# A hybrid encoder layer: input products of un-normalised h, the norm's factor applied after PSUM

## The chip, the cores and the metric

The kernel runs on one core of a Trainium2 chip. A core has five engines with queues of their own: TensorE (PE: matrix products and transposes, into PSUM), VectorE (DVE), ScalarE (ACT), GpSimd (POOL), and SyncE (SP), which here issues all DMAs. SBUF is the on-chip memory; PSUM holds the results of products in banks. The metric is device microseconds (us) of one execution; lower is better.

## The reference

One layer on h, 16 meta tokens and 512 tokens of 1024 channels, all float32:

```python
u = rmsnorm(h, norm_mix)                      # h * rsqrt(mean(h*h) + eps) * gain
proj = u @ w_in
gates = sigmoid(proj[..., C_RW + C_FX:] + b_gate)
y_rw = rwkv7_branch(proj[..., :C_RW], ...)    # f + mu * (token_shift(f) - f), then a recurrence over tokens
y_fx = fox_branch(proj[..., C_RW:C_RW + C_FX], ...)   # q, k normed per head; softmax attention with forgetting
merged = gates[..., :1024] * (y_rw @ w_out_rw) + gates[..., 1024:] * (y_fx @ w_out_fx)
h = h + merged @ w_o
h = h + square(relu(rmsnorm(h, norm_mlp) @ w_up)) @ w_down
```

The factor of rmsnorm is one number for each token, and a product is linear in u; so it can be applied to h before the product, or to each column of the product after it.

## The kernel before

Channels lie on partitions, tokens along the free dimension (528 columns, two halves of 264). A product in float32 accuracy is made of three passes: every operand is split into a high part and a remainder (`uhi`/`ulo` for u, `whi`/`wlo` for a weight block of 128 outputs), and hi·hi, hi·lo and lo·hi add up in one PSUM bank. A block of the input projection is thus 8 x 3 products for each half of the tokens.

**Front.** x arrives in two halves of tokens. It is scaled by the norm's gain and split; with this un-normalised split the eight forget logits (`pf`) and two blocks, the inputs of the low-rank decay (`B_LORA`) and of the output gate (`B_GD`), are multiplied (`proj`), and `rs`, the norm's factor, is made from the squares (`pss`). Then h is multiplied by `rs` and split a second time, into the same `uhi`, `ulo` (lines 369 to 376). All later blocks use this one. The two first blocks become `lhi`/`llo` after tanh; the first recurrent product, `pup` (line 682), reads them.

**Middle.** 24 blocks for four pairs of heads (FoX q, k, v and recurrent k, r, v for each) and 16 gate blocks, taken by `projections` from a list in order of rank (recurrent 1, FoX 2, gates 9). A FoX or recurrent block has two parts of 264 columns, a q or gate block one of 512. Each part goes to one of two PSUM banks named pj; a function `evac` takes it out. For a recurrent block `evac` is the token shift (`tshift`, lines 300 and 301): ACT writes the product times mu, shifted by one token, and DVE adds the product times 1-mu; both read PSUM. A gate is written to DRAM and read back at the output projection.

For each of two groups of two pairs the recurrence goes: decay (`pup`), norm of the keys (`pkk`), scores of chunks of 64 tokens (`psr`, into `Bm` and `L`), keys turned (`pbt`), the inverse of a triangular matrix for each chunk (`inverse`: 15 substitution steps on DVE for blocks of 16, then products `pw`, `pw2`), then `chain`, nine steps that depend on each other (`pch`, `pyy`), and group norm (`pyt`, `pg`). FoX attention of one pair goes over four blocks of 128 queries: scores (`psc`), softmax on DVE and ACT, transposes (`ppt`, `ppm`), and the mix (`py`).

**What sets the order.** PE's order in the middle is written out when the program is built: `Turns` picks, by rank, the stream whose next products are ready by the estimates of `Clock`, and otherwise goes on with a product of the projection. `Clock` estimates each instruction by engine, fixed cost and size. The other engines' orders come from the framework's scheduler, with `high_priority` for ranks 0 and 1. Engines run in order; waits are semaphores.

**Output projection and the rest.** For each of eight blocks m of 128 channels, two gates are loaded (`gl`, two buffers for each branch), go through tanh, and multiply the products `po` (DVE, line 1036); POOL adds the two branches (line 1038), and ACT and DVE split the sum (lines 1039, 1040). Then come `w_o`, the second norm and the MLP, in which PE's order is that of the code.

## Time and profile before

| | us |
|---|---|
| median of 3 runs (lowest to highest) | 927.95 (926.56 to 931.89) |
| the profiled execution | 923.5 |
| its span | 921.7 |
| busy PE / weight loads / DVE / ACT / POOL | 872.5 / 709.4 / 523.7 / 424.9 / 159.9 |
| front: to the first recurrent product | 41.3 |
| middle: to the first product of the output projection | 475.3 |
| output projection, w_o, MLP | the rest, 446.4 |

The profile names an instruction by line, engine and `output<-inputs`, with a count (x4). PE is busy nearly all the time by the page, but a product's end is modelled, and small products and half a clock count as busy too; so the table of stretches is read together with the waits. "PEclk" is the share of full clock that PE was granted. In a list of waits stand the waiting engine, tile and line, the releaser after the arrow, total us, number and longest.

### The profile page before, as it was taken

The page shows a single profiled execution, that of the slowest core. Times are in us where ns is not written, and L with a number is a line of the kernel's source. Part 1 is how long each engine was busy: PE and PEld are TensorE (multiplying, and loading weights), DVE is VectorE, ACT ScalarE, POOL GpSimd, SP SyncE. Part 2 cuts the span into 40 slices and gives each one's busy share as a digit, 9 for nine tenths or more (in the row PEclk, how much of TensorE's full clock was granted, in tenths as well). Part 3 has the DMA queues.
Part 4 walks back from the last instruction along what each step waited for, and adds up shares of the span by engine and source line. Part 5 has one row for each costly group of instructions (what it writes and reads, how often), then busy time and mean ns, then how long its engine had stood idle before and what let it go on. Part 6 is the DMA issues. An engine that isn't in the chain of part 4 may idle for free.

```text
span 921.7 us, 15446 instructions
## 1 busy us (share of the span) xinstructions
PE 872.5 (95%) x5964; PEld 709.4 (77%) x5964; DVE 523.7 (57%) x1052; ACT 424.9 (46%) x887; POOL 159.9 (17%) x145
## 2 busy tenths in 40 slices
PE   6589898999998999999989999999999999999998
PEld 4587785768896777676768878988888888888886
DVE  7966885465887893565387664454423245452322
ACT  7755352686465533674465553344322234442221
POOL 4253433123343352112102100000000000000000
PEclk9889998999999999999989999999999999999999
DMA  6121204022111142211266540132323232322331
GB/s 207 46 71 47 69 27 132 25 71 70 50 46 59 47 133 70 69 60 47 69 229 205 183 160 1 58 103 92 101 94 101 94 102 93 100 95 94 123 116 57
DMA packets 45449, 83.30 MB, mean 90 GB/s; under 512 B 5048, under 2 KB 6200, under 8 KB 45376
## 3 DMA queue, kind: packets, MB, share of 16 engines
q1 hardware_dynamic: 45376, 82.32, 26.8%
q8 instruction: 47, 0.77, 0.3%
q14 instruction: 26, 0.21, 0.1%
HBM read 75.99 MB, written 6.31 MB: 89 GB/s over the span
## 4 chain that ended last, share of the span: by engine, by line
PE 76%; DVE 15%; DMA 3%; ACT 3%; issue 2%; POOLq 0%; POOL 0%; SPq 0%; DVEq 0%; ACTq 0%
PE po L1117 19%; PE pd L1150 19%; PE pj L472 18%; PE po L1083 2%; PE po L1034 2%; PE pw L824 2%; PE psc L576 1%; PE py L621 1%; DVE tmp L806 1%; DMA wraw<-in_wup 1%; DVE AX L818 1%; DVE xt L373 1%; PE pbt L772 1%; DVE AX L807 1%; DMA wraw<-in_win 1%
## 5 line engine op out<-in xcount | busy, mean ns | idle before, releaser
L233 DVE TENSOR_TENSOR wlo<-wraw,whi 128x512 fp32r<-128x512 f32 x148 | 107.0, 724 | 171.6 <-ACT whi L232 170.1
L232 ACT CAST whi<-wraw 128x512 fp32r<-128x512 f32 x152 | 93.8, 620 | 190.4 <-PE pd L1150 109.6
L472 PE MATMUL pj<-uhi,whi 128*128 128x264 f32 (+1 forms) x480 | 168.5, 351 | 9.5 <-DVE orr L301 4.7
L472 PE MATMUL pj<-uhi,wlo 128*128 128x264 f32 (+1 forms) x480 | 156.3, 326 | 0.0
L472 PE MATMUL pj<-ulo,whi 128*128 128x264 f32 (+1 forms) x480 | 156.3, 326 | 0.0
L444 POOL TENSOR_TENSOR wlo<-wraw,whi 128x512 fp32r<-128x512 f32 x80 | 109.1, 1367 | 216.8 <-ACT whi L443 201.4
L472 PEld LDWEIGHTS pj<-uhi,whi 128*128 128x128 f32 x480 | 92.4, 192 | 30.6 <-issue 10.9
L1150 PE MATMUL pd<-whi,fhi 128*128 128x512 f32 x256 | 99.6, 389 | 0.0
L1150 PE MATMUL pd<-wlo,fhi 128*128 128x512 f32 x256 | 99.6, 389 | 0.0
L1150 PE MATMUL pd<-whi,flo 128*128 128x512 f32 x256 | 99.6, 389 | 0.0
L472 PEld LDWEIGHTS pj<-uhi,wlo 128*128 128x128 f32 x480 | 92.6, 193 | 7.2
L472 PEld LDWEIGHTS pj<-ulo,whi 128*128 128x128 f32 x480 | 92.7, 193 | 4.3
L1117 PE MATMUL po<-zhi,whi 128*128 128x512 f32 (+1 forms) x248 | 94.8, 382 | 0.0
L1117 PE MATMUL po<-zlo,whi 128*128 128x512 f32 (+1 forms) x248 | 94.8, 382 | 0.0
L1117 PE MATMUL po<-zhi,wlo 128*128 128x512 f32 (+1 forms) x248 | 94.8, 382 | 0.0
L443 ACT CAST whi<-wraw 128x512 fp32r<-128x512 f32 x80 | 49.4, 618 | 51.9 <-PE pj L472 27.5
L1150 PEld LDWEIGHTS pd<-whi,fhi 128*128 128x128 f32 x256 | 48.0, 188 | 10.1
L1150 PEld LDWEIGHTS pd<-wlo,fhi 128*128 128x128 f32 x256 | 48.0, 188 | 10.0
L1150 PEld LDWEIGHTS pd<-whi,flo 128*128 128x128 f32 x256 | 48.0, 188 | 9.9
L1117 PEld LDWEIGHTS po<-zlo,whi 128*128 128x128 f32 x248 | 46.6, 188 | 9.1
L1117 PEld LDWEIGHTS po<-zhi,whi 128*128 128x128 f32 x248 | 46.6, 188 | 9.0
L1117 PEld LDWEIGHTS po<-zhi,wlo 128*128 128x128 f32 x248 | 46.6, 188 | 9.0
(279 smaller groups left out, 1455.6 us busy)
## 6 DMA issues: line engine op xcount, KB each, us to landing
wraw<-in_win SPq DMA_DIRECT2D x84, 256.0 KB, 2.6
wraw<-in_wup SPq DMA_DIRECT2D x64, 256.0 KB, 2.6
wraw<-in_wdn SPq DMA_DIRECT2D x64, 256.0 KB, 2.6
gd<-gt SPq DMA_DIRECT2D x16, 256.0 KB, 2.1
wraw<-in_wout SPq DMA_DIRECT2D x16, 256.0 KB, 3.3
gl<-gd SPq DMA_DIRECT2D x16, 256.0 KB, 3.1
wraw<-in_wo SPq DMA_DIRECT2D x16, 256.0 KB, 3.2
xt<-in_ht SPq DMA_DIRECT2D x8, 264.0 KB, 4.7
```

The lines of the kernel that those rows point to most:

```text
L232: A.copy(hi, raw)
L233: low.tensor_tensor(lo, raw, hi.bitcast(F32), ALU.subtract)
L373: V.scalar_tensor_tensor(xt[t][:, k, :], xt[t][:, k, :], pr[:, C_GN + k:C_GN + k + 1], rss[t], ALU.mult, ALU.mult)
L443: A.copy(hi, raw)
L444: G.tensor_tensor(lo, raw, hi.bitcast(F32), ALU.subtract)
L472: mm(po, a, b[:, k, a0:a1], start=n == 0, stop=n == 23)
L576: mm(sc, q[hs, 128 * i:128 * i + 128], k[hs, a:b], start=True, stop=True)
L824: mm(ps_[hs, n - b0, :], lhs(n)[hs], rhs(n)[hs], start=True, stop=True)
L1034: mm(po, a, b[:, k, :], start=n == 0, stop=n == 11)
L1083: mm(po, a[:, k, 128 * i:128 * i + 128], b[:, k, :], start=n == 0, stop=n == 23)
L1117: mm(po[:, t0:t1], a, b[:, k, t0:t1], start=n == 0, stop=n == 23)
L1150: mm(pd[i], a[:, b_, 128 * i:128 * i + 128], b, start=b_ == 0 and n == 0, stop=b_ == 15 and n == 2)
```

## The change

h times gain is split once and used un-normalised by all input products; the second pass over h and its split are gone. The factor `rs` stays in SBUF for all 528 tokens and is applied after PSUM: in the token shift (DVE, then ACT and DVE over 528 columns), on FoX q, k and v (POOL), and on the gates when they are read back (POOL, before tanh). Every part leaves PSUM by one ACT copy. In the front the two first blocks and the forget logits are multiplied together, channel block by channel block, with the weights loaded between the pieces of x; the four weight differences there go from POOL to DVE. `manual_schedule`, which keeps PE's order as written, now spans the front too.

In the planner, a DVE operation in SBUF alone costs 0.2 more and a transpose half as much. In the inverse, four of the eight final copies go from DVE to ACT, the products wait for the pieces that they read instead of for the whole tile, and other streams get turns between the substitution steps. The tile `dg` shares a buffer with `lc`, and the keys are turned before the next pair's decay.

```diff
-                    cost = n / 600 if big else n / 1200
+                    cost = n / 600 if big and not x.is_transpose else n / 1200
...
+                    if eng == "DVE" and not any(a.tensor.space == PSUM for a in ins + outs):
+                        fixed += 0.2
...
-        def tshift(blk, dst):
-
-            tm = rp.tile([128, 1 + T], F32, name="tm")
-            V.memset(tm[:, 0:1], 0.0)
+        def tshift(blk, dst, **kw):
+
+            raw = rp.tile([128, 1 + T], F32, **(kw or dict(name="tm")))
+            V.memset(raw[:, 0:1], 0.0)
+
+            def finish():
+                f = raw[:, 1:]
+                V.tensor_tensor(f, f, rs, ALU.mult)
+                act(dst, f, AF.Copy, scale=pr1[:, blk:blk + 1])
+                V.scalar_tensor_tensor(dst, raw[:, :T], pr[:, C_MU + blk:C_MU + blk + 1], dst, ALU.mult, ALU.add)
 
             def evac(po, sl):
-                act(tm[:, sl.start + 1:sl.stop + 1], po, AF.Copy, scale=pr[:, C_MU + blk:C_MU + blk + 1])
-                V.scalar_tensor_tensor(dst[:, sl], po, pr1[:, blk:blk + 1], tm[:, sl], ALU.mult, ALU.add)
+                A.copy(raw[:, 1 + sl.start:1 + sl.stop], po)
+                return finish if sl.stop == T else None
             return evac
+
+        manual = st.enter_context(ExitStack())
+        manual.enter_context(tc.manual_schedule(engines={mybir.EngineType.PE}))
...
+            def load_x(t, c):
+                nc.sync.dma_start(xt[t][:, 2 * c:2 * c + 2, :].rearrange("p a b -> p (a b)"), ht[t, c])
+            load_x(0, 0)
+            w2 = [[], []]
+            for j in range(2):
+                for i, blk in enumerate((B_LORA, B_GD)):
+                    w2[i].append(load_h(win[blk][:, 512 * j:512 * j + 512], V, "w", (4, 4, 4)))
+                load_x(0, 1 + j)
+            load_x(0, 3)
             for c in range(4):
-                nc.sync.dma_start(xt[0][:, 2 * c:2 * c + 2, :].rearrange("p a b -> p (a b)"), ht[0, c])
-            w_lora = load_w(win[B_LORA], (G, G))
-            for c in range(4):
-                nc.sync.dma_start(xt[1][:, 2 * c:2 * c + 2, :].rearrange("p a b -> p (a b)"), ht[1, c])
-            w_gd = load_w(win[B_GD], (G, G))
+                load_x(1, c)
...
-            rss = []
+            V.tensor_scalar(pr1, pr[:, C_MU:C_MU + 14], -1.0, 1.0, ALU.mult, ALU.add)
+            shifts = [tshift(12 + blk, lfs[i], name="tl", tag="ov", bufs=2) for i, blk in enumerate((B_LORA, B_GD))]
             for t in range(2):
                 tk = slice(HT * t, HT * t + HT)
-                for c in range(4):
-                    sq = xp.tile([128, 2, HT], F32, name="sq", bufs=3)
-                    act(sq, xt[t][:, 2 * c:2 * c + 2, :], AF.Square)
-                    for k in range(2 * c, 2 * c + 2):
-                        gn = pr[:, C_GN + k:C_GN + k + 1]
-                        act(uhi[:, k, tk], xt[t][:, k, :], AF.Copy, scale=gn)
-                        V.scalar_tensor_tensor(ulo[:, k, tk], xt[t][:, k, :], gn, uhi[:, k, tk].bitcast(F32), ALU.mult, ALU.subtract)
-                    if c == 0:
-                        acc = xp.tile([128, HT], F32, name="acc")
-                        V.tensor_tensor(acc, sq[:, 0, :], sq[:, 1, :], ALU.add)
-                    else:
-                        for k in range(2):
-                            V.tensor_tensor(acc, acc, sq[:, k, :], ALU.add)
                 pf = psm("pf")[:8, :HT]
+                pls = [ppj("pj") for i in range(2)] if t == 0 else [ps.tile([128, 512], F32, name="p" + b, tag=b, bufs=1) for b in ("py", "ch")]
+                pls = [x[:, :HT] for x in pls]
+                acc = xp.tile([128, 2, HT], F32, name="acc")
                 n = 0
                 for k in range(KB):
-                    for a, b in passes([x[:, 8 * k:8 * k + 8] for x in wf], U):
-                        mm(pf, a, b[:, k, tk], start=n == 0, stop=n == 23)
+                    if k % 2 == 0:
+                        c = k // 2
+                        sq = acc if c == 0 else xp.tile([128, 2, HT], F32, name="sq", bufs=2)
+                        act(sq, xt[t][:, k:k + 2, :], AF.Square)
+                        if c > 0:
+                            V.tensor_tensor(acc, acc, sq, ALU.add)
+                    gn = pr[:, C_GN + k:C_GN + k + 1]
+                    act(uhi[:, k, tk], xt[t][:, k, :], AF.Copy, scale=gn)
+                    V.scalar_tensor_tensor(ulo[:, k, tk], xt[t][:, k, :], gn, uhi[:, k, tk].bitcast(F32), ALU.mult, ALU.subtract)
+                    for j in range(3):
+                        for a, b, dst, cols in [(*passes([x[:, 8 * k:8 * k + 8] for x in wf], U)[j], pf, tk)] + [(*passes(wk(w2[i], k), U)[j], pls[i], tk) for i in range(2)]:
+                            mm(dst, a, b[:, k, cols], start=n == 0, stop=n == 23)
                         n += 1
                 pq = psm("pss")[:, :HT]
-                mm(pq, ones, acc, start=True, stop=True)
-                rs = xp.tile([128, HT], F32, name="rs")
-                act(rs, pq, AF.Ln, bias=eps, scale=1.0 / 1024)
-                act(rs, rs, AF.Exp, scale=-0.5)
-                rss.append(rs)
-                V.tensor_tensor(f0[:, tk], pf, rs[:8], ALU.mult)
-                if t == 0:
-                    V.tensor_scalar(pr1, pr[:, C_MU:C_MU + 14], -1.0, 1.0, ALU.mult, ALU.add)
-                    shift = tshift(12 + B_LORA, lfs[0])
-
-                def normed_shift(po, sl):
-                    V.tensor_tensor(po, po, rss[sl.start // HT], ALU.mult)
-                    shift(po, sl)
-
-                proj(B_LORA, normed_shift, ((tk.start, tk.stop),), w_lora)
-            shift = tshift(12 + B_GD, lfs[1])
-            proj(B_GD, normed_shift, w=w_gd)
-            for t in range(2):
-                tk = slice(HT * t, HT * t + HT)
-                for c in range(4):
-                    for k in range(2 * c, 2 * c + 2):
-                        V.scalar_tensor_tensor(xt[t][:, k, :], xt[t][:, k, :], pr[:, C_GN + k:C_GN + k + 1], rss[t], ALU.mult, ALU.mult)
-                    kk = slice(2 * c, 2 * c + 2)
-                    A.copy(uhi[:, kk, tk], xt[t][:, kk, :])
-                    V.tensor_tensor(ulo[:, kk, tk], xt[t][:, kk, :], uhi[:, kk, tk].bitcast(F32), ALU.subtract)
+                for j in range(2):
+                    mm(pq, ones, acc[:, j, :], start=j == 0, stop=j == 1)
+                act(rs[:, tk], pq, AF.Ln, bias=eps, scale=1.0 / 1024)
+                act(rs[:, tk], rs[:, tk], AF.Exp, scale=-0.5)
+                for finish in [shifts[i](pls[i], tk) for i in range(2)]:
+                    if finish:
+                        finish()
+                V.tensor_tensor(f0[:, tk], pf, rs[:8, tk], ALU.mult)
...
+                        ck.read()
+                        ck.urgent = True
+                        with tc.high_priority():
+                            finish = evac(po, slice(a0, a1))
+                        ck.read()
+                        ck.urgent = rank < 2
+                        if finish:
+                            with tc.high_priority() if ck.urgent else nullcontext():
+                                finish()
+                        ck.read()
+                        ck.urgent = False
...
-                    act(gt, po, AF.Identity, bias=pr[:, C_BG + i:C_BG + i + 1])
+                    A.copy(gt, po)
...
+                            G.tensor_tensor(f, f, rs[:, c0:], ALU.mult)
+                            d["s"] = act(sq[:, c0:], f, AF.Square)
+
                         def evac(po, sl):
-                            d["s"] = act(sq[:, sl], po, AF.Square)
                             A.copy(f[:, sl.start - c0:sl.stop - c0], po)
+                            return finish if sl.stop == T else None
...
-                    return lambda po, sl: A.copy(d["v"][:, sl], po)
+                    v = d["v"]
+
+                    def evac(po, sl):
+                        A.copy(v[:, sl], po)
+                        return (lambda: G.tensor_tensor(v, v, rs, ALU.mult)) if sl.stop == T else None
+                    return evac
...
-                self.dg = dg = rp.tile([128, NCH, 64], F32, name="dg")
+                self.dg = dg = rp.tile([128, NCH, 64], F32, name="dg", tag="lc")
...
+                if s % 2:
+                    yield lambda: ck.ready(AX_) - 3.5
...
-            for dst, src in ((Tt2, TT), (Dn, At)):
-                for qd in range(4):
-                    rs_ = slice(32 * qd, 32 * qd + 32)
-                    o = 32 * (qd % 2)
-                    V.tensor_copy(dst[rs_, :, o:o + 32], src[rs_, :, :n2].rearrange("p t n -> p n t"))
+            for qd in range(4):
+                rs_ = slice(32 * qd, 32 * qd + 32)
+                o = 32 * (qd % 2)
+                A.copy(Dn[rs_, :, o:o + 32], At[rs_, :, :n2].rearrange("p t n -> p n t"))
+                V.tensor_copy(Tt2[rs_, :, o:o + 32], TT[rs_, :, :n2].rearrange("p t n -> p n t"))
...
-                yield lambda: max(ck.ready(Dn), banks(1))
+                yield lambda: max(at, banks(1))
                 p1 = six("pw", b0, lambda n: Bms[n // NCH][:, n % NCH, :64], lambda n: Dn[:, n, :])
                 V.tensor_tensor(W2[:, b0:b0 + 6, :], p1, bc(mask16, 1, 6), ALU.mult)
+                w2_at.append(now(W2))
             for b0 in range(0, n2, 6):
-                yield lambda: max(ck.ready(W2), banks(2))
+                yield lambda: max(w2_at[b0 // 6], banks(2))
...
-            yield lambda: max(ck.ready(Dn, Tt2), banks(2))
-            pws = [psm("pw")[:, :NCH * 32].rearrange("p (a b) -> p a b", b=32) for pr_ in range(2)]
             for pr_ in range(2):
+                yield lambda: max(d_at[1 + pr_], banks(1))
...
+                    yield from q.keys_turned()
                     if j == 0:
                         yield from prs[1].decay()
-                    yield from q.keys_turned()
...
-                act(g, g, AF.Tanh, scale=0.5)
+                G.tensor_tensor(g, g, rs[:, NM:], ALU.mult)
+                act(g, g, AF.Tanh, bias=bgh[:, 8 * br + m:8 * br + m + 1], scale=0.5)
```

51 lines of the change are left out of this document (27 added, 24 removed).

## The prediction

> **What bounds the kernel now.** I read the table of stretches first, then what TensorE (PE) waited for between 42 and 475 us, then the chain of waits and the timeline at the places the change touches. In rows of stretches the columns are length, then busy us (and count) of PE, weight loads, VectorE (DVE), ScalarE (ACT), GpSimd (POOL), then granted PE clock, DMA share, GB/s.
>
> ```profile
> 36.00:48.00 12.00, 6.74 (x36) 6.51 (x37) 10.03 (x18) 7.45 (x12) 1.30 (x4) 0.57 0.14 45
> 60.00:64.00 4.00, 1.40 (x11) 1.20 (x11) 3.97 (x8) 0.48 (x1) 1.34 (x3) 1.00 0.38 130
> 64.00:68.00 4.00, 4.00 (x22) 3.90 (x20) 3.11 (x5) 1.29 (x2) 2.75 (x5) 0.57 0.00 0
> 150.00:157.00 7.00, 5.52 (x35) 3.69 (x36) 2.03 (x11) 3.71 (x9) 3.77 (x3) 0.52 0.44 147
> 475.00:520.00 45.00, 44.66 (x197) 36.98 (x198) 33.64 (x44) 26.87 (x46) 10.17 (x7) 1.00 0.68 228
> ```
>
> PE works without a break from 475 us on; before that it stands still at a few places, and about half a clock follows each long one (0.57, 0.57, 0.52). These are the waits:
>
> ```profile
> PE pup L682 <- DVE llo L257: 7.7, 1, 7.7
> PE pj L472 <- DVE orr L301: 4.7, 2, 2.6
> PE pj L472 <- ACT gt L483: 4.3, 1, 4.3
> PE psr L757 <- DVE L L761: 4.1, 5, 1.2
> PE pch L889 <- DVE Rs L885: 2.7, 2, 2.2
> PE psr L757 <- DVE BK L716: 2.3, 1, 2.3
> ```
>
> The largest (columns: us in total, times, longest) ends the front; the next two are input products that found no free bank because one had not left PSUM. So the stage up to 475 us is PE's work plus such stops, and products of the input projection (pj) fill between the steps of the recurrence.
>
> **Front.** Removed are 16 L373 and 8 L376 passes on DVE and 8 on ACT that normalise h and split it again:
>
> ```profile
> L373 DVE SCALAR_TENSOR_TENSOR xt<-xt,pr,rs 128x264 f32<-128x264 f32 x16 | 10.1, 662 | 0.0
> L376 DVE TENSOR_TENSOR ulo<-xt,uhi 128x528 fp32r<-128x528 f32 x8 | 5.5, 694 | 0.0
> 5.65 0.39 PE L349 MATMUL pf<-uhi,wf 128*8 128x264 f32 x1 [5.65 <-ACT uhi L337]
> 13.93 2.10 PE pj L287 x17
> 41.26 1.47 PE pup L682 x6
> 42.73 11.06 PE pj L472 x72
> ```
>
> On PE, before, pup (the decay product, from lhi and llo) stands ahead of every pair product:
>
> ```order
> L287 MATMUL pj<-uhi,whi 128x264
> L287 MATMUL pj<-ulo,whi 128x264
> L287 MATMUL pj<-uhi,wlo 128x264
> L682 MATMUL pup<-lhi,lw_464 128x264 x2
> L682 MATMUL pup<-llo,lw_464 128x264 x2
> ```
>
> After the change, on PE at the same place (L468 is the pair products, L698 pup):
>
> ```order
> L468 MATMUL pj<-uhi,whi 128x264
> L468 MATMUL pj<-ulo,whi 128x264
> L468 MATMUL pj<-uhi,wlo 128x264
> L698 MATMUL pup<-lhi,lw_423 128x264 x2
> L698 MATMUL pup<-llo,lw_423 128x264 x2
> ```
>
> 36 pair products now come ahead of pup. The front's own 144 products (48 pf, 96 of the two blocks) take 2.10/17 = 0.124 us each, 17.9 in all, from 5.65; with 1 us for the doubled sum of squares and 3 for weights and the slow start they end near 27.5 (bounds 24.5 and 33.5, where PE stops now). 36 x 0.124 = 4.5 us of pair products bring PE to 32. Then it waits for llo again, whose line is rs, token shift, tanh, split:
>
> ```profile
> 24.98 0.48 ACT L354 ACTIVATE rs<-pss,eps 128x264 f32<-128x264 f32 x1 [0.25 <-PE pss L352]
> 29.20 1.28 ACT L401 ACT_TABLE_LOAD   x1
> 40.20 0.61 ACT L256 CAST lhi<-lf 128x528 fp32r<-128x528 f32 x1
> ```
>
> From 27.5: Ln and Exp 1.0, DVE product 0.7, ACT copy 0.6, DVE sum 0.7, two table loads 2.6, four ACT passes 2.6, cast and difference 1.3, hops 1: pup at 38. That is 3.3 us earlier with 4.5 us of work already done: **-7.8** (bounds -11 and -4). The half clock behind this stop stays, since 6 us of idling is left of 7.7. SP issues the same loads of x and weights in another order, all ahead of PE's need; POOL's four weight differences move to DVE (2.8 at the 0.69 of L376), less than the 15.6 that DVE loses.
>
> **Evacuation and the recurrence.** A token-shifted block left PSUM by two ACT and two DVE passes of 264; now ACT copies alone, and DVE, ACT, DVE follow over 528:
>
> ```profile
> L301 DVE SCALAR_TENSOR_TENSOR orr<-pj,pr,tm 128x264 f32<-128x264 f32 x8 | 3.9, 491 | 2.3 <-ACT tm L300 2.1
> 59.63 1.64 DVE L726 SCALAR_TENSOR_TENSOR L<-okk,P 64x567 f32<-64x567 f32 x1
> 61.37 0.75 DVE L726 SCALAR_TENSOR_TENSOR L<-okk,P 64x567 f32<-64x567 f32 x1
> 62.90 0.49 DVE L301 SCALAR_TENSOR_TENSOR orr<-pj,pr,tm 128x264 f32<-128x264 f32 x1
> ```
>
> Here the wait is plain: the pass of 0.49 that frees the bank stood behind four long ones. Without DVE in that path the 4.7 goes. The 4.3 of gt goes if the copy is put early on ACT; ACT itself was held by a load there:
>
> ```profile
> 149.49 0.30 ACT L256 CAST lw<-lraw 128x128 fp32r<-128x128 f32 x1 [6.68 <-DMA lraw<-in_lora]
> 150.75 0.68 ACT L483 ACTIVATE gt<-pj,pr 128x512 f32<-128x512 f32 x1
> ```
>
> So -9 of waits (bounds -9 and -4.7), and the half clock behind them: 4 us at 0.57 and 7 at 0.52 with 4.0 and 5.5 busy, some 4.4. The new planner costs (0.2 us more for a DVE pass that stays in SBUF, so more filler ahead of psr) and the inverse waited for piece by piece should take 5 of the other waits (9.1 for psr and pch above). Against it: each block's data are ready 0.7 + 0.65 + 0.75 - 0.49 = 1.6 us later, 12 x 1.6 = 19 us if nothing covered it; pair products cover it wherever they are left, so I take +2. Sum **-16.4**, bounds -22 and 0. The inverse's copies are at:
>
> ```profile
> 138.68 3.62 DVE L818 COPY Tt<-TT 32x576 f32<-32x576 f32 x3
> 142.32 3.85 DVE L818 COPY AX<-AX 32x576 f32<-32x576 f32 x4
> ```
>
> ACT now does the last 3.85 beside DVE. PE has products meanwhile, so I count nothing; without that cover it would be a gain of about 4 for each of two inverses, which the lower bound takes in. The 12 new POOL products of FoX (about 1.3 each) lie behind the same filler.
>
> Where the page has DVE passes with two SBUF inputs beside POOL, one took 1.64 where its twin took 0.75, and L301, which reads PSUM, kept 0.49. [...]
>
> The tile dg now shares lc's buffer, so the next pair's decay comes after the keys are turned; its products stand among filler, and I count nothing, or up to 2 us of chain without it.
>
> **The end of the stage.** On PE, before, the last attention block (psc, ppt, py) and group norm (pyt, pg) run after the recurrent chain, with filler:
>
> ```order
> L576 MATMUL psc<-ka,qa 128x272 x2
> L472 MATMUL pj<-uhi,whi 128x512
> L472 MATMUL pj<-ulo,whi 128x512
> L472 MATMUL pj<-uhi,wlo 128x512
> L618 MATMUL py<-pTm,vm 64x128 x2
> L621 MATMUL py<-pT,vt 64x128 x2
> ```
>
> After the change, on PE from the same score product (L592):
>
> ```order
> L592 MATMUL psc<-ka,qa 128x272 x2
> L917 MATMUL pch<-Rs,Tt 64x64 x4
> L634 MATMUL py<-pTm,vm 64x128 x2
> L637 MATMUL py<-pT,vt 64x128 x2
> L970 MATMUL pyt<-cs,y_rw 64x128 x4
> ```
>
> The chain (pch) now ends inside the attention block and no filler is left.
>
> ```profile
> 431.99 0.68 DVE L926 TENSOR_REDUCE st<-y_rw 128x8 f32<-128x512 f32 x1
> 438.77 0.69 DVE L935 TENSOR_TENSOR y_rw<-y_rw,rsgy 128x512 f32<-128x512 f32 x1
> 445.54 0.52 PE L576 MATMUL psc<-ka,qa 64*128 64x144 f32 x4
> 464.27 2.77 PE L576 MATMUL psc<-ka,qa 64*128 64x272 f32 x8
> 475.34 0.50 PE L1034 MATMUL po<-yhi,whi 128*128 128x512 f32 x1 [0.36 <-ACT y_fx L622]
> ```
>
> Today first score to last is 18.7 us, and 11.1 more to po. DVE's 7.5 us of group norm (431.99 to 439.5) came before; now it and two chain steps stand in that stretch. With them the last scores come some 27 us after the first (18.7 + 7.5, and some of the steps): 38 in all instead of 29.8. The chain's last step falls some 10 us after the first score. About 1 us of PE work has moved ahead of it. **+9** (bounds +4 and +12).
>
> **The output projection.** A gate needs an extra POOL pass (L1057) before tanh, 16 in all. POOL, before:
>
> ```order
> L1038 TENSOR_TENSOR gl0_5609<-gl0_5609,gl1_5626 128x512
> L1038 TENSOR_TENSOR gl0_5658<-gl0_5658,gl1_5675 128x512
> L1038 TENSOR_TENSOR gl0_5707<-gl0_5707,gl1_5724 128x512
> L1038 TENSOR_TENSOR gl0_5756<-gl0_5756,gl1_5773 128x512
> L1038 TENSOR_TENSOR gl0_5805<-gl0_5805,gl1_5822 128x512
> ```
>
> POOL, after (L1057 scales a gate, L1067 adds the two branches):
>
> ```order
> L1067 TENSOR_TENSOR gl0_5588<-gl0_5588,gl1_5606 128x512
> L1057 TENSOR_TENSOR gl1_5708<-gl1_5708,rs_67 128x512
> L1057 TENSOR_TENSOR gl0_5690<-gl0_5690,rs_67 128x512
> L1067 TENSOR_TENSOR gl0_5639<-gl0_5639,gl1_5657 128x512
> L1057 TENSOR_TENSOR gl1_5759<-gl1_5759,rs_67 128x512
> L1057 TENSOR_TENSOR gl0_5741<-gl0_5741,rs_67 128x512
> ```
>
> The sum of block m+1 (gl0_5639) now waits behind the gate of m+2 (gl0_5690), which takes the buffer that block m (gl0_5588) frees.
>
> ```profile
> 481.97 1.79 POOL L1038 TENSOR_TENSOR gl<-gl,gl 128x512 f32<-128x512 f32 x1 [37.73 <-DVE gl L1036]
> 483.80 0.63 ACT L1039 ACTIVATE mhi<-gl 128x512 fp32r<-128x512 f32 x1 [1.38 <-POOL gl L1038]
> 484.46 0.69 DVE L1040 SCALAR_TENSOR_TENSOR mlo<-gl,mhi 128x512 fp32r<-128x512 f32 x1
> 487.33 1.29 POOL L1038 TENSOR_TENSOR gl<-gl,gl 128x512 f32<-128x512 f32 x1 [3.57 <-DVE gl L1036]
> 488.61 0.63 ACT L1029 ACTIVATE gl<-gl 128x512 f32<-128x512 f32 x1 [1.13 <-DMA gl<-gd]
> 519.54 0.68 DVE L1036 SCALAR_TENSOR_TENSOR gl<-gl,po 128x512 f32<-128x512 f32 x1
> 520.74 0.68 DVE L1036 SCALAR_TENSOR_TENSOR gl<-gl,po 128x512 f32<-128x512 f32 x1
> ```
>
> A round is mhi 0.63, mlo 0.69, load 3.46 (485.15 to 488.61), gate 1.29, sum 1.29, hops 0.2: 7.6 us, against 45/8 = 5.6 for PE's block. The first sum ends about 9 us after po starts; four rounds later it is 39, and two more gates and sums (with the load of gate 7) bring the last gate's product to about 52, where 520.74 + 0.68 is 46. PE runs ahead by four banks, so it loses only what shows at the end, where the next product needs those banks. **+7** (bounds +3, every overlap found; +17, each POOL pass at 1.79 and a half clock after the stop).
>
> From the products after po to the end no instruction changes: 0.
>
> **Sum.** -7.8 - 16.4 + 9 + 7 = -8.2. The profiled execution took 923.5 us (span 921.7), so 915.3 on its scale; the median of the runs, 927.95, lies 4.4 above it, so 920.
>
> **Rivals.**
> - The gate loop is hidden (the scheduler's gaps let POOL catch up, +1) and evacuation gives its full -19: 927.95 - 7.8 - 19 + 9 + 1 = 911. For it: PE has four banks of slack; against: the order on POOL is fixed.
> - The end of the stage and the loop give it all back, evacuation half of it (-8, gt's wait stays): -7.8 - 8 + 9 + 7, no change, 928. For it: ACT was held by a load, not by its own work, and now every block hangs on ACT.
> - Slower: the recurrent chain becomes the bound. It ran from pup at 41.3 to 431, 390 us, and its end no longer has filler behind it. Add 19 us of later blocks and, at 0.4 us each, 24 x 0.4 = 10 of DVE passes that meet POOL; take off 8 for the inverses and 3.3 for the front: it ends at 449. From there the rest of the 38 us, 28, lead to po: 477, then +7: 927.95 + 8 = 936. It decides once the chain ends past 445. For it: DVE is full where PE stops (3.97 of 4 us from 60 on). Against: in the 390 us the chain often waited for PE's filler, and the first psr waits are short.
>
> **Chances.** Forecast 0.46 (own range 910 to 923), hidden loop 0.17, no change 0.15, chain as the bound 0.22. Half a per cent, 4.6 us, is about what a measurement can tell from no change; so faster 0.63, same 0.15, slower 0.22. The range goes from 904, with a better evacuation than any single case, to 936, where the slow case ends.
>
> **What would show it.** pup near 38 us with 36 pair products ahead of it; no wait of pj on DVE; po starting near 460 instead of 475, with PE idle between attention's last scores; POOL sums 7 to 8 us apart after 480 and a stop of PE before the next product. Wrong if pup stays at 41, if psr waits grow past 15 us in total, or if the sums come 5.5 us apart.

## The result and the profile after

The changed kernel takes 959.75 us (median of four runs, 957.97 to 961.21), the kernel before, run beside it, 927.75 us: a ratio of 1.0336 with an interval of 1.0297 to 1.0375. The change makes the kernel slower; the forecast was 920 us. The profiled execution's span is 956.4 us, against 921.7.

Three points of the trace cut the span into the parts that the prediction summed. First PE at pup, the first score product of the last attention block (view of one line: min, median and longest duration, then first and last start), and the first product of the output projection, po, all of the changed kernel:

```profile
37.96 0.59 PE L698 MATMUL pup<-lhi,lw 64*128 64x264 f32 x2 [5.89 <-ACT lhi L261]
```

```profile
L592 PE MATMUL psc<-ka,qa x20: 282/434/782, 458.7 to 487.7; 64*128 64x272 f32 x8, 64*128 64x144 f32 x4, 64*128 64x400 f32 x4, 64*128 64x256 f32 x4
```

```profile
497.08 0.80 PE L1063 MATMUL po<-yhi,whi 128*128 128x512 f32 x1 [0.36 <-ACT y_fx L638]
```

| from the traces, us | before | forecast | after |
|---|---|---|---|
| pup starts | 41.3 | 38 | 38.0 |
| first score of the last attention block | 445.5 | 421 | 458.7 |
| from there to po | 29.8 | 38 | 38.4 |
| po to the end | 446.4 | 453 | 459.3 |

(421 is 445.5 - 7.8 - 16.4.) The front and the end of the stage came as forecast, the output projection lost twice what was forecast, and between pup and the last attention block 21 us were lost where 16 should have been won: 458.7 - 38.0 against 445.5 - 41.3 is 16.5 us longer, in spite of 36 pair products (4.5 us) already done.

What PE waited for in the changed kernel up to 500 us (total, times, longest):

```profile
PE psr L773 <- DVE L L777: 7.4, 4, 4.2
PE pup L698 <- ACT lhi L261: 5.9, 1, 5.9
...
PE psr L773 <- DVE BK L732: 5.6, 2, 3.8
PE ppt L621 <- DVE rsum L607: 5.5, 1, 5.5
PE pyt L970 <- DVE y_rw L963: 4.7, 1, 4.7
...
PE psr L773 <- DVE nm L603: 2.2, 1, 2.2
```

The waits of pj on orr and on gt (9 us before) are gone, as the change meant. In their place psr, the recurrent pairs' score product, waits 15.4 us in all (7.4 before, smaller rows than those shown included), and two products of the attention and the group norm 5.5 and 4.7. The table of stretches shows the clock that was granted behind such stops. Before, then after (columns as in the prediction):

```profile
60.00:125.00 65.00, 56.95 (x453) 47.95 (x454) 47.50 (x85) 30.80 (x60) 25.75 (x27) 0.97 0.17 55
240.00:345.00 105.00, 99.33 (x749) 82.45 (x748) 89.31 (x189) 51.61 (x116) 43.43 (x37) 1.00 0.21 70
```

```profile
60.00:125.00 65.00, 56.48 (x398) 47.52 (x397) 42.72 (x63) 30.56 (x57) 30.87 (x27) 0.85 0.16 50
240.00:345.00 105.00, 96.03 (x735) 79.82 (x737) 73.13 (x159) 55.46 (x126) 45.59 (x40) 0.92 0.17 53
```

From 60 to 125 us PE is as busy as before but gets 398 products done instead of 453. Summed from the trace's clock records, 70.6 us up to po ran at half clock, 30.7 before. The whole stretch up to po, before and after:

```profile
0.00:475.34 475.34, 430.99 (x3941) 342.53 (x3941) 325.44 (x761) 264.10 (x609) 148.12 (x137) 0.97 0.23 75
```

```profile
0.00:497.08 497.08, 444.85 (x3944) 356.50 (x3944) 310.00 (x724) 276.42 (x621) 159.16 (x145) 0.93 0.23 73
```

Of the 21.7 us by which po comes later, PE is busy 13.9 us longer, with practically the same number of products, and stands still 7.9 us longer. So the greater part of this loss shows as longer busy time, with the clock halved for 39.9 us more, and not as the stops themselves; ends of products are modelled, so the split is rough.

What lies ahead of the first psr stop (61.7 to 65.5 us) is on DVE and POOL, each in a fence:

```profile
57.88 0.74 DVE L742 SCALAR_TENSOR_TENSOR L<-okk,P 64x567 f32<-64x567 f32 x1
58.55 1.26 DVE L743 TENSOR_SCALAR L<-okk 64x9 f32<-64x9 f32 x1
59.82 0.75 DVE L742 SCALAR_TENSOR_TENSOR L<-okk,P 64x567 f32<-64x567 f32 x1
60.49 1.27 DVE L743 TENSOR_SCALAR L<-okk 64x9 f32<-64x9 f32 x1
61.77 1.78 DVE L731 SCALAR_TENSOR_TENSOR BK<-okk,lc 128x576 f32<-128x576 f32 x1
63.66 1.75 DVE L732 SCALAR_TENSOR_TENSOR BK<-tha,BK 128x576 f32<-128x576 f32 x1
```

```profile
57.99 1.79 POOL L746 TENSOR_TENSOR sq<-orr,sg 128x512 f32<-128x512 f32 x1 [3.14 <-DVE okk L727]
...
60.00 2.94 POOL L440 TENSOR_TENSOR wlo<-wraw,whi 128x512 fp32r<-128x512 f32 x2
63.64 2.80 POOL L750 TENSOR_TENSOR dg<-cs,P 64x576 f32<-64x576 f32 x2 [0.69 <-DVE BK L731]
```

A DVE pass of nine elements (L743) takes 1.26 us here, and each of the long ones lies beside a POOL pass. By groups, the same passes over the whole stage (count, busy, mean ns), L727 before being L743 after:

```profile
L727 DVE TENSOR_SCALAR L<-okk 64x9 f32<-64x9 f32 x8 | 2.9, 362 | 0.0
```

```profile
L294 DVE TENSOR_TENSOR tm<-tm,rs 128x528 f32<-128x528 f32 x12 | 13.6, 1130 | 11.6 <-ACT tm L299 11.6
L777 DVE TENSOR_TENSOR L<-psr,cs 64x384 f32<-64x384 f32 x24 | 13.1, 554 | 0.4
L743 DVE TENSOR_SCALAR L<-okk 64x9 f32<-64x9 f32 x8 | 9.0, 1128 | 0.0
```

The new scaling pass L294 averages 1.13 us: six of the twelve took 0.68 to 0.71 us, five took 1.62 to 1.68, and each of these five began while a POOL pass was running; so did the twelfth, of 1.10, and one of the six short ones (0.69 at 259.02). L777, which reads PSUM, took 0.54 to 0.56 in all 24 passes, 12 of which lie beside a POOL pass.

In the output projection POOL's sums (L1067) and gates (L1057) of the changed kernel, and where PE stops at its end:

```profile
505.01 1.29 POOL L1067 TENSOR_TENSOR gl<-gl,gl 128x512 f32<-128x512 f32 x1
509.11 1.30 POOL L1057 TENSOR_TENSOR gl<-gl,rs 128x512 f32<-128x512 f32 x1 [2.81 <-DMA gl<-gd]
510.98 1.29 POOL L1057 TENSOR_TENSOR gl<-gl,rs 128x512 f32<-128x512 f32 x1 [0.57 <-DMA gl<-gd]
512.22 1.74 POOL L1067 TENSOR_TENSOR gl<-gl,gl 128x512 f32<-128x512 f32 x1
...
519.89 1.30 POOL L1067 TENSOR_TENSOR gl<-gl,gl 128x512 f32<-128x512 f32 x1
```

```profile
547.59 0.50 PE L1095 MATMUL po<-whi,mhi 128*128 128x512 f32 x1 [1.49 <-ACT whi L237]
549.28 0.78 PE L1095 MATMUL po<-wlo,mhi 128*128 128x512 f32 x1 [1.19 <-DVE wlo L238]
553.57 0.80 PE L1095 MATMUL po<-whi,mhi 128*128 128x512 f32 x1 [1.80 <-DVE gl L1065]
```

The sums come 7.2 and 7.7 us apart, and PE stands before the next product.

### The profile page after: what moved, and what is told of

It is laid out like the page before. It is cut to its first block, busy times and chain, and to the rows that moved or that the text cites. A ratio compares the mean times of both kernels' runs of the same rounds, so it can differ in the third digit from the quotient of the medians.

```text
span 956.4 us, 15455 instructions
## 1 busy us (share of the span) xinstructions
PE 892.9 (93%) x5968; PEld 725.9 (76%) x5968; DVE 508.6 (53%) x1013; ACT 438.9 (46%) x899; POOL 193.4 (20%) x169
## 4 chain that ended last, share of the span: by engine, by line
PE 62%; DVE 8%; ACT 5%; POOL 3%; DMA 2%; issue 1%; POOLq 0%; DVEq 0%; ACTq 0%; SPq 0%
PE po L1146 18%; PE pd L1179 18%; PE pj L468 11%; PE po L1095 2%; PE po L1112 2%; DMA gl<-gd 2%; POOL gl L1057 1%; PE py L637 1%; POOL gl L1067 1%; PE psc L592 1%; DVE tmp L824 1%; PE pw L842 1%; ACT L256 1%; PE ppt L623 1%; PE pch L917 1%
## 5 line engine op out<-in xcount | busy, mean ns | idle before, releaser
L238 DVE TENSOR_TENSOR wlo<-wraw,whi 128x512 fp32r<-128x512 f32 x152 | 109.4, 721 | 184.5 <-ACT whi L237 183.0
L468 PE MATMUL pj<-uhi,whi 128*128 128x264 f32 (+1 forms) x480 | 171.0, 356 | 0.2 <-ACT qa L519 0.2
L468 PE MATMUL pj<-uhi,wlo 128*128 128x264 f32 (+1 forms) x480 | 158.9, 331 | 0.5 <-POOL wlo L440 0.5
L468 PE MATMUL pj<-ulo,whi 128*128 128x264 f32 (+1 forms) x480 | 159.1, 331 | 0.0
L468 PEld LDWEIGHTS pj<-uhi,whi 128*128 128x128 f32 x480 | 94.5, 197 | 20.5 <-issue 10.6
L468 PEld LDWEIGHTS pj<-uhi,wlo 128*128 128x128 f32 x480 | 94.8, 198 | 8.2 <-POOL wlo L440 0.7
L468 PEld LDWEIGHTS pj<-ulo,whi 128*128 128x128 f32 x480 | 95.1, 198 | 4.8
```

The source lines that it names most:

```text
L238: low.tensor_tensor(lo, raw, hi.bitcast(F32), ALU.subtract)
L468: mm(po, a, b[:, k, a0:a1], start=n == 0, stop=n == 23)
```

## The experiments

Ratios are against the kernel before, run on the same chip in the same set. "po" is where the output projection starts in the profiled run. The kernel before took 927.75 us in the set of the result and 929.2 to 932.1 in the later sets, so a difference of two medians from different sets is good to some 4 us only.

**Which part is lost where.** The planner's figures put back:

```diff
-if eng == "DVE" and not any(a.tensor.space == PSUM for a in ins + outs):
-    fixed += 0.2
-cost = n / 600 if big and not x.is_transpose else n / 1200
+cost = n / 600 if big else n / 1200
-yield lambda: ck.ready(AX_) - 3.5
...
```

> The changed kernel (959.75 us) with the planner's costs, the head start of the inverse and the assumed time of lhi and llo put back to those of the kernel before (927.75). Theory order (the planner's new figures put PE's products in a worse order): the stage up to the output projection gets most of its 21.7 us back, 945 us or less. Theory late data (the keys' token shift now lies in SBUF, its passes meet POOL's, and psr is late whatever the planner thinks): 956 to 964 us, psr waits still 12 us or more in total (15.4 now). Theory gate loop (the output projection alone): 957 to 962.

952.19 us, ratio 1.0217 (1.0180 to 1.0253); po at 490.2, psr still waits 14.0 us. The time lies between the ranges of the theories: the planner's new figures cost some 7 us, not the 15 of the theory of order, and psr's waits do not come from them. But when psr comes does: the last pair's first psr starts at 315.5 instead of 340.0, and the last pch, the chain's last step, at 430.9, as in the kernel before (429.5; 468.2 in the changed kernel), while po is still 15 us later than there. When the chain ends does not set po alone.

The gates scaled before they are stored:

```diff
-A.copy(gt, po); nc.sync.dma_start(gates_d[i], gt)
+A.copy(gt, po); finish: G.tensor_tensor(gt, gt, rs[:, NM:], ALU.mult); nc.sync.dma_start(gates_d[i], gt)
-G.tensor_tensor(g, g, rs[:, NM:], ALU.mult)     (in the output projection)
```

> The changed kernel with the gates multiplied by rs by POOL before they are stored, so that the output projection's loop has no extra POOL pass. Theory gate loop: from the first po to the end falls from 459 us to about 446 (before: 446), 946 to 950 us in all; the sixteen POOL passes in the stage before lie behind filler. Theory that the output projection loses time to something else (weights, the halved clock on entry): from po to the end stays within 2 us of 459, 957 to 962 us. Theory late data: the earlier stage gets worse by up to 5 us from more POOL passes beside DVE's, whatever the loop gives.

949.36 us, ratio 1.0177 (1.0129 to 1.0225). From po to the end 448.0 us, 11.3 less than in the changed kernel; po itself starts 2.7 later. POOL's sums in that run:

```profile
506.96 1.62 POOL L1070 TENSOR_TENSOR gl<-gl,gl 128x512 f32<-128x512 f32 x1 [38.63 <-DVE gl L1068]
512.26 1.29 POOL L1070 TENSOR_TENSOR gl<-gl,gl 128x512 f32<-128x512 f32 x1 [3.69 <-DVE gl L1068]
```

They are 5.3 us apart again. The gate pass in the loop is nearly all of the loss of the output projection.

The token shift scaled by DVE on the way out of PSUM:

```diff
-A.copy(raw[:, 1 + sl.start:1 + sl.stop], po)
+V.tensor_tensor(raw[:, 1 + sl.start:1 + sl.stop], po, rs[:, sl], ALU.mult)
-V.tensor_tensor(f, f, rs, ALU.mult)
```

> The changed kernel with the token-shifted blocks leaving PSUM through DVE, which multiplies by rs on the way out (one pass fewer, the copy on ACT is gone), as the kernel before had a DVE pass there. Theory late data (SBUF-only DVE passes beside POOL and one pass more make psr late): psr waits fall from 15.4 to 9 us or less, 944 to 953 us. Theory that freeing the banks by ACT alone is worth it: pj waits on DVE come back (9 us before), 960 to 968 us. Theory order or gate loop: 956 to 962.

943.03 us, ratio 1.0121 (1.0077 to 1.0165), po at 481.6: 15.5 us of the stage come back, by an edit that gives up "ACT alone". Its scaling passes, by groups:

```profile
L298 DVE TENSOR_TENSOR tm<-pj,rs 128x264 f32<-128x264 f32 x24 | 10.3, 431 | 10.8 <-PE pj L467 10.6
```

Two of them take 0.86 us where L294 took 1.13; the five from 42 to 72 us took 0.42 or 0.43, the one at 55.96 within a POOL pass of 1.75. But psr waits 13.6 us still, so the reason that the theory gave, shorter psr waits, is not what the run shows.

**Is the chain behind psr the bound?** Each pair's first psr due 4 us later in the planner, in both kernels:

```diff
-yield lambda: max(ck.ready(BK, *L) if c0 == 0 ...
+yield lambda: max(ck.ready(BK, *L) + 4.0 if c0 == 0 ...
```

> The changed kernel with the first score product of each recurrent pair due 4 us later in the planner, so that PE gets about 4 us more of input products ahead of psr. Theory late data with PE's order fixed too early: psr waits fall from 15.4 us to 3 or less, the halved clock behind them (64.6 to 81.7 and 269.4 to 283.1 us) goes, 943 to 951 us. Theory that the recurrent chain itself is the bound: each of four pairs ends 4 us later and there is no gain, 962 to 975 us.

> The kernel before (927.75 us) with the same edit that made the changed kernel 16.2 us slower (four times 4.05): the first score product of each recurrent pair due 4 us later in the planner. Theory that only the change made the chain of work behind psr the bound (po starts 178 us after the fourth psr in the kernel before, 157 in the changed one): 928 to 935 us, po at 475 to 481. Theory that this chain bounds both kernels alike: 940 to 946.

The changed kernel: 975.99 us, ratio 1.0471 (1.0432 to 1.0511), 16.2 us more than without by the medians, 12.5 by the ratios. Its waits:

```profile
PE pyt L970 <- DVE y_rw L963: 14.0, 2, 8.4
...
PE pv L562 <- POOL vf L550: 5.7, 2, 4.8
...
PE psr L773 <- DVE L L777: 5.6, 4, 2.8
PE pj L468 <- ACT vf L549: 5.2, 2, 4.4
```

psr waits 7.4 us now, as in the kernel before, and what stood behind it in PE's order waits instead. The kernel before: 946.12 us, ratio 1.0165 (1.0122 to 1.0207), some 15 to 17 us more. So four delays of 4 us at psr cost the total about their sum in both kernels; filler hides them in neither, and the change alone did not make the kernel sensitive there. But the planner then orders everything behind psr anew: in the kernel before the four first psr come 4, 7, 26 and 32 us later, not 4, 8, 12 and 16. What one delay costs at its own stop is not shown.

**Both edits, and more of the kind.** The edits of the second and third run together; then the planner's old figures as well:

> The changed kernel with both edits that helped alone: the token-shifted blocks are scaled by rs on DVE as they leave PSUM, and the gates are scaled before they are stored. Theory that the two losses lie in separate stretches and add: 959.75 - 16.7 - 10.4 = 932.6, so 929 to 937 us, with po to the end at 447 to 449 and po starting at 482 to 486. Theory that early gates' POOL passes meet the DVE passes that the first edit helped: po starts past 490 and the sum is 940 or more.

> The same with the planner's figures of the kernel before as well. Theory that the new planner figures cost time of their own (6.9 us up to po, alone): 922 to 930 us. Theory that they and the SBUF token shift hurt at the same stops, so that with one mended the other costs nothing: 929 to 937, within 3 us of the run without this edit.

937.20 us, ratio 1.0081 (1.0046 to 1.0116): the gains nearly add (932.6 by the sum). With the old planner figures 946.39, 1.0152 (1.0090 to 1.0214): 9 us worse by the medians, where the same edit alone won 7.6. Its four runs spread from 936.9 to 948.5 and the two intervals just overlap, so a loss is likely but not certain; that the edit wins its 6.9 us here as well, as the first theory has it, is not so.

Every product scaled on DVE from PSUM (FoX and gates too); the inverse's Dn copies on DVE; both:

```diff
-G.tensor_tensor(f, f, rs[:, c0:], ALU.mult)
-A.copy(f[:, sl.start - c0:sl.stop - c0], po)
+V.tensor_tensor(f[:, sl.start - c0:sl.stop - c0], po, rs[:, sl], ALU.mult)
...
-A.copy(Dn[rs_, :, o:o + 32], ...)
+V.tensor_copy(Dn[rs_, :, o:o + 32], ...)
```

> The changed kernel with every input product scaled by rs on DVE as it leaves PSUM: token shift, FoX and gates. No ACT copy and no POOL pass for rs is left. Theory that POOL's passes beside DVE's SBUF passes, and ACT's copies, cost time in the stage before po beyond the token shift's part: po starts at 470 to 478 (481.6 with the token shift alone), 918 to 928 us in all. Theory of the change (banks must be freed by ACT alone, DVE is late): pj waits on DVE of 8 us or more return, 935 us or more. Theory that the token shift was all of it: 933 to 940, as with early gates on POOL (937.2).

> The run with token shift scaled from PSUM and early gates (937.2 us) with the four copies of the inverse's Dn back on DVE instead of ACT. The prediction counted nothing for them. Theory that ACT's four copies (4.8 us, one behind another) hold up the softmax's exp, on which PE's ppt waits 5.9 us at 358: that stop goes to 2 us or less, 928 to 933 us. Theory that the inverse then ends as much later and PE waits for it instead: 935 to 941.

> Both edits: every product scaled by rs on DVE from PSUM, and Dn's copies on DVE. If both theories of cost hold, the sum of the two gains: 910 to 922 us, faster than the kernel before (927.75). If DVE then has too much in the recurrent chain: 930 us or more, with waits on DVE over 20 us up to po.

940.11 us, 1.0123 (1.0083 to 1.0164); 941.29, 1.0134 (1.0097 to 1.0171); 936.15, 1.0072 (1.0044 to 1.0101). None brings a gain that can be told, all three lie within some 4 us of the run that they start from (937.2): for rs in FoX and the gates the third theory comes nearest, that the token shift was all of it, and for the copies the second; and for both together the theory of too much on DVE, with psr, ppt and pyt waiting 33.0 us for DVE up to po. The 5.9 us stop of ppt that was to go with the copies became 7.5.

**What rs costs at all.**

> The changed kernel (959.75 us) with every multiplication by rs after the front left out, and nothing else changed: outputs are those of un-normalised h in the token shift of the pairs, FoX and the gates. Theory that these passes are the loss: the gate loop's 11 us and nearly all of the token shift's go, 918 to 930 us. Theory that the loss lies in ACT's copies and in PE's order: 940 us or more, the 11 us of the gate loop aside nothing.

932.52 us, ratio 1.0035 (1.0010 to 1.0059), po at 480.1, po to the end 450.6: 27 us, 17 of them before po. The edit takes the factor from the front's two blocks too, which go through the same token shift: pup starts at 34.1 instead of 38.0, so 3.9 of the 17 us lie in the front. Even without the passes it is not faster than the kernel before. Two more parts taken out of it in turn, the shared dg and the planner's figures:

> The changed kernel with every multiplication by rs after the front left out (932.5 us; the outputs are those of un-normalised h), and dg in a buffer of its own with the next pair's decay ahead of the keys' turn, as in the kernel before. Theory that the shared dg, which cost nothing in the kernel before but moved its fourth psr from 297 to 311, holds the changed kernel's chain: fourth psr at 318 or earlier instead of 331, 918 to 925 us. Theory that it costs nothing here either: 929 to 936.

> The same with the planner's figures of the kernel before as well, so that of the change there remain the front, ACT's evacuation without rs, the inverse's products in pieces and its copies on ACT. Theory of the prediction's terms (front -7.8, waits of pj gone, inverse a gain of 6 as run alone): 908 to 916 us. Theory that ACT's evacuation over the whole width costs the chain what the front gives: 920 to 930. Theory that any order of PE the planner makes from wrong costs differs by 8 us either way: no further gain over the run without this edit, or a loss.

930.73 us, 1.0036 (1.0006 to 1.0065): the last pair's first psr comes at 316.9 instead of 331, and nothing is won. Then 924.75, 0.9951 (0.9928 to 0.9973), with po at 474.5: the planner's old figures win 6 us here, and some 9 us stay above what the prediction's own terms give (916 at most).

**Single parts in the kernel before.** The shared dg with the later decay; the inverse in pieces; the same with Dn's copies on DVE:

> The kernel before (927.75 us) with one part of the change alone: dg shares lc's buffer and the next pair's decay comes after the keys are turned. My prediction counted nothing for it. Theory that it is one of the causes (dg then waits until DVE has read lc, POOL's two dg passes fall on the BK passes ahead of psr, and the next pair's pup starts some 10 us later): pup of the second pair at 80 us or later instead of 74, 933 to 942 us. Theory of the prediction, that filler covers it: 925 to 931 us.

> The kernel before (927.75 us) with the inverse of the change alone: four copies on ACT, each product waited for by its own piece, and the head start of the steps. The prediction took 5 us of gain for this and the planner's costs together. Theory of the prediction: 921 to 926 us. Theory that ACT's four copies hold up what ACT must free (the wait of pj on gt, 4.3 us at 147): 930 to 936 us. No effect: 926 to 930.

> The kernel before with the inverse in pieces (921.5 us), but Dn's four copies on DVE as the kernel before has them. Theory that the gain is the pieces' and the copies on ACT cost what they save (5 us stop of pj on gt at 147): 917 to 922 us, faster than both kernels. Theory that the gain is the copies' (DVE is free 3.85 us earlier): 925 to 929.

928.42 us, 0.9975 (0.9954 to 0.9995): no cost. 921.48, **0.9921 (0.9888 to 0.9954): 0.8% less than the kernel before**. 935.31, 1.0061 (1.0036 to 1.0086): with the copies on DVE the gain is gone, so by these two runs it is ACT's copies that earn it, not the pieces. The first theory was the wrong way round, and that the rest alone costs 6 us was in neither.

**The clock, and the meeting of DVE and POOL.** Ten products of constants ahead of each pair's psr, into a bank that psr overwrites, PE's order otherwise unchanged:

```diff
+for _ in range(10): mm(raws[0][:, :384], ident, cs[:, :384], start=True, stop=True)
```

> The changed kernel (959.75 us) with ten products of constants (about 3 us, into the bank that the first psr overwrites) ahead of each pair's psr, PE's order otherwise the same: they run in the stops that are there anyway (3.8, 1.7, 4.1, 2.2 us). Theory that the halved clock behind the stops carries half of the loss up to po (70.6 us of it, 30.7 in the kernel before): half clock falls to 50 us or less, po at 489 to 493, 951 to 956 us. Theory that the loss is the waiting itself: half clock or not, psr starts no earlier, and the products add what the stops are shorter than they (1.3 and 0.8 us): 959 to 964 us.

963.95 us, 1.0369 (1.0311 to 1.0427), po at 500.5. Half clock up to po falls to 46.7 us, and the stretch of 60 to 125 us runs at full clock:

```profile
60.00:125.00 65.00, 62.85 (x455) 50.48 (x454) 44.49 (x65) 31.63 (x60) 32.93 (x30) 1.00 0.17 49
```

455 products by the trace, 40 of them of constants, against 398, and yet po is 3.4 us later. But the constants are not free. The trace records each as two, and ten take 6.61 us, not the 3 that were expected:

```profile
61.59 6.61 PE L420 MATMUL psr<-cs 128*128 128x384 f32 x20
```

So psr starts later, not as before: at 68.1 instead of 65.5 for the first pair. Up to po the constants take 28.2 us of PE; its other products take 13.3 us less than in the changed kernel (431.6 against 444.9), and it stands still 11.5 less (40.7 against 52.2). The two gains and the cost nearly cancel. This run therefore does not show whether the halved clock is a cause of the loss or only a mark of it.

Last, the weight differences wlo from POOL to DVE:

```diff
-G.tensor_tensor(lo, raw, hi.bitcast(F32), ALU.subtract)
+V.tensor_tensor(lo, raw, hi.bitcast(F32), ALU.subtract)
```

> The changed kernel with the weight differences wlo (80 passes, 1.3 us on POOL, 0.7 on DVE) moved from POOL to DVE. Theory that DVE's passes held up by POOL's (0.16 to 1.26, 0.75 to 1.75 ahead of psr) are the cost of the SBUF token shift: those passes run at their short times, psr waits fall from 15.4 to 8 us or less, and in spite of 55 us more DVE work 945 to 955 us. Theory that the cost is the number of steps from product to psr and DVE's own load: DVE later still, 965 us or more.

933.49 us, ratio 1.0041 (1.0017 to 1.0065): 26 us less than the changed kernel, with 80 passes more on DVE, and less than any theory gave. po starts at 472.4, before the 475.3 of the kernel before; what remains is the gate loop, 461.0 us from po to the end. Its groups on DVE:

```profile
L440 DVE TENSOR_TENSOR wlo<-wraw,whi 128x512 fp32r<-128x512 f32 x77 | 57.3, 752 | 30.3 <-ACT whi L439 23.2 <-PE ppt L623 6.6
...
L294 DVE TENSOR_TENSOR tm<-tm,rs 128x528 f32<-128x528 f32 x12 | 8.4, 702 | 2.2 <-ACT tm L299 2.1
...
L743 DVE TENSOR_SCALAR L<-okk 64x9 f32<-64x9 f32 x8 | 3.5, 444 | 0.0
```

L294 is back from 1130 to 702 ns, L743 from 1128 to 444. DVE's busy time grows by 28.8 us only (508.6 to 537.4), though the 77 passes of this stage alone are 57.3. psr waits 11.2 us, not the 8 expected. POOL is busy 54 us up to po instead of 159, so whatever waits for POOL can also come sooner. The planner reckons the moved passes too, so PE's order is not that of the changed kernel, and not all of the 26 us need be the meeting of DVE and POOL. The edit was not tried in the kernel before, nor together with early gates.

## Why the prediction was wrong

**Front, -7.8: right.** pup at 38.0, with 36 pair products ahead of it, after a stop of 5.9 us (6 forecast).

**Evacuation and recurrence, -16.4: the step that failed.** Its first part held: no product waits on DVE for a bank any more, nor on gt. The clock and the other waits did not follow: the half clock that was to shrink by some 4.4 us of loss grew from 30.7 to 70.6 us, and psr, whose waits were to fall, waits 15.4 us instead of 7.4 (the prediction names more than 15 as a sign that it is wrong). And what failed above all is the sentence on the other side: each block's data "are ready ... 1.6 us later, 12 x 1.6 = 19 us if nothing covered it; pair products cover it wherever they are left, so I take +2". By the table, the last attention block starts 13.2 us later than before; without the front's 7.8 that is +21 in place of -16.4, outside the bounds of -22 and 0. Two things were wrong in it. Filler does not cover what comes late at psr: four delays of 4 us cost 12 to 17 in the two kernels. And the lateness was larger than 1.6 us, since the new passes read and write SBUF alone and meet POOL's: scaling from PSUM gave back 15.5 us up to po, and taking POOL's weight differences out of DVE's way 24.7. Of these gains 12.6 and 13.5 us are PE's busy time (432.3 and 431.3 us up to po instead of 444.9), with the half clock at 41.0 us in both runs: the clock that goes with the stops belongs to the loss, and how much of it that clock causes is not shown.

The prediction had the row for this (1.64 us at 59.63, with POOL passes until 60.67, where its twin took 0.75) and left it out of the sum. The runs show more of the kind: 1130 ns for L294 in the changed kernel against 702 with the weight differences off POOL, and 554 for L777, which reads PSUM, though half of its passes lie beside POOL's. The nine-element L743, which has one input, was longer beside POOL as well: seven of its eight passes began within a POOL pass and took 1.25 to 1.30 us; the eighth, with none beside it, took 0.17.

**Inverse, 0 for the copies, and 5 us with the planner: not a fixed price.** In the kernel before the new inverse wins some 7 us (0.8%), with its copies on DVE it loses 6; in the changed one, on top of the two cures, moving the copies changed nothing that could be told. The planner's figures cost 7.6 alone and 6 with rs left out, and seem to win beside the two cures. **Shared dg, 0: right**, in the kernel before and with rs left out.

**End of the stage, +9: right, in part by luck.** 29.8 became 38.4; the last scores start 29 us after the first (27 forecast), the chain's last step 9.5 after it (10 forecast), and pyt waits for the group norm on DVE. But 16 us of this stretch ran at half clock, 6.8 before, which the forecast did not count.

**Output projection, +7: right in kind, too small.** The loop's round is 7.2 to 7.7 us, as worked out (7.6). But the last gate product ends at 553.5 (552.83 and 0.69), 56.4 after po, where 52 was forecast; and the next block's weights are late as well (the stops of 1.49 and 1.19 above). 12.9 us, of which the gate pass is 11.3.

**The slower rival, 936, named the nearest mechanism**: later blocks, and DVE passes that meet POOL at 0.4 us each. The 0.4 for all 24 passes was an estimate, and no run shows it: L294's excess is near it, 1130 - 702 = 428 ns, but the twelve of L296 average 805 where the two in the front took 750. And it priced the 24 new passes alone: L743, an old one, now meets POOL's too (362 to 1128 ns, 6 us over eight passes), since the whole sequence has shifted against POOL's. The chain's last step starts 38.7 us later, where the rival has 18. But it is not the bound by itself: with rs left out it starts at 466.3, nearly as late as in the changed kernel, and po comes 17 us sooner.

**What stays open.** With rs left out, dg in its own buffer and the old planner figures the kernel takes 924.75 us, while front and inverse alone should give some 914 (927.75 - 7.8 - 6). How lateness at psr becomes time at po is open: a psr that came 14 us sooner won nothing (dg in its own buffer), and an end of the chain as early as before left po 15 us late (the planner's old figures). And the planner's edit, which wins in two neighbours and seems to lose in a third, suggests that any new order of PE is worth several us either way; a single edit of a few us in this stage may measure no more than that.

## What to carry to other kernels

Before moving a step from a pass that reads PSUM to one that works in SBUF alone, look at what POOL runs at that time: here the same multiplication cost 0.43 us for 264 columns from PSUM (mean of 24) and 1.13 instead of 0.70 for 528 in SBUF. An engine with many short helper passes, off the critical path itself, can be the cause of a late chain on another engine; moving them onto the busier engine was the best cure tried (26 us here, with PE's order changed as well). And that filler hides a delay is a claim to test before it goes into a sum at nothing: delay the step by a known amount, here four times 4 us, which cost 12 to 17. A filling that is to keep the clock up must be priced too: ten products of constants took 6.6 us here, where 3 were expected.

## What the runs showed of the hardware

PE stayed at half clock from 64.6 to 81.7 us of the changed kernel, though by the profile it was busy 16.13 of those 17.10 us:

```profile
64.60:81.70 17.10, 16.13 (x81) 12.26 (x81) 11.21 (x20) 6.02 (x10) 5.81 (x7) 0.50 0.14 44
```

With ten products of constants from 61.6 to 68.2 us, over the stop ahead of it, the same stretch kept the full clock (12 of the 131 are records of the constants):

```profile
64.60:81.70 17.10, 16.18 (x131) 12.03 (x131) 12.12 (x21) 8.32 (x17) 5.90 (x7) 1.00 0.14 41
```

The halved stretches in the traces of the kernel before and the changed kernel last 3.41 to 17.07 us, all multiples of 3.41 us, up to the one that the end of the trace cuts off (2.47 and 3.14). Of the five lengths of 3.41 us from 64.6 to 81.7, PE was busy 3.37 of 3.41 us in the third and 3.42 of 3.42 in the fourth by the profile, and the fifth ran at half clock as well. What brings the full clock back is not shown by these traces.
